# Modulation products in plain float32 on quarters of TensorE's columns, in a two-layer hybrid diffusion block

## The chip, the core and the metric

The kernel runs on one core of a Trainium2 chip. Its five engines are named in the profile's way: PE (TensorE, the matrix engine; PEld its weight loads), DVE (VectorE), ACT (ScalarE), POOL (GpSimd) and SP (SyncE, which only issues transfers here). The metric is the device time of one execution in microseconds, the median of several. A profiled execution also has a span, from its first to its last instruction.

## The reference

Two layers of one trunk work on 256 context tokens and 512 latent tokens of 1024 features, all in float32. Each layer computes a modulation vector of 6 x 1024 values for each of the two token groups from that group's condition (`c` for the latents, `c_ctx` for the context). The six parts are shift, scale and gate of the mixers, and shift, scale and gate of the MLP:

```python
for layer in range(DEPTH):
    ctx_out = layer < DEPTH - 1
    mods = jax.nn.silu(c.astype(f32)) @ mod_w[layer] + mod_b[layer]
    sh1, sc1, gt1, sh2, sc2, gt2 = jnp.split(mods[:, None, :], N_MOD, axis=-1)
    cmods = jnp.split(jax.nn.silu(c_ctx.astype(f32)) @ mod_w[layer] + mod_b[layer], N_MOD)

    p_lat = (rmsnorm(x, norm_mix[layer]) * (1.0 + sc1) + sh1) @ w_in[layer]
    p_ctx = (rmsnorm(ctx, norm_mix[layer]) * (1.0 + cmods[1]) + cmods[0]) @ w_in[layer]
    ...
    x = x + gt1 * (jnp.concatenate([ya_l, yb_l, yc_l], axis=-1) @ w_out[layer])

    h = rmsnorm(x, norm_mlp[layer]) * (1.0 + sc2) + sh2
    x = x + gt2 * sq_relu_mlp(h, mlp_w1[layer], mlp_w2[layer])
    ...
return rmsnorm(x, norm_final)
```

What is left out are the three mixers, S5, gated DeltaNet and RWKV-7, each on its own columns of `p`, and the same steps for the context with `cmods` in layer 0. The products with `mod_w` have only two rows on one side, one for each token group, and 25 MB of weights for each layer on the other.

## The kernel before

Activations are kept with features on the partitions. Dense products (`product`, line 290, whose matmul is line 296) are made exact by splitting both sides into two float32r parts each, high and low: three matmuls in place of one. `weight` (line 265) loads 128 rows by 512 columns of weights into a `wl` tile (line 271), ACT casts the high part into `wh` (line 272), and DVE or POOL subtracts for the low part in `wo` (line 273). Each of the three names has three buffers (`wide`, line 223). Products of plain float32 are two matmul instructions each in the trace.

The order on every engine's queue is made ahead of time: what is emitted has a class of urgency, `CHAIN` (the recurrences) first, then `LEVEL`, `READ`, `PREP`, `S5`, `DENSE`, `FILL`, and a planner places each instruction by modelled times. On an engine the order is then fixed, and an instruction that waits holds all behind it. Tiles of one name are handed out in the order of emission; the banks "d" of PSUM, two of them, serve dense products, modulation and S5 alike.

Modulation is `mods` (line 908). For each group of 512 of the 6144 columns it goes over the eight row tiles of the contraction, sums into one "d" bank, copies the sums to SBUF (line 929), turns them into columns with four transposes (line 932) and adds the bias (line 934). At the start (`eng` None, called at line 1185) four groups of layer 0 are made in plain float32: the weights are loaded to tiles of the arena (line 921), and the stationary side is `sc[:, k]`, two columns (line 922). The projection `front` of layer 0 needs these groups. Everywhere else (`mods` in `run`, line 1195, with 'v') weights are split by `weight` with the low part on DVE, and each row tile takes two float32r matmuls, line 925 with four columns (high and low of both token groups) and line 926 with two; line 936 adds the second pair of rows. There are 20 such groups: six right after the first projection, emitted between pieces of S5 (`next(self.more)`), four ahead of the context's output projection, two inside the context's MLP, and eight in layer 1. All are of class `DENSE`.

The other lines that matter: line 990 loads the tokens, lines 952, 320 and 323 make the norms' reciprocals, 807 to 885 are S5, lines 1708 to 1733 and 1488 to 1511 the recurrences of RWKV-7 and DeltaNet, line 398 and 404 blocks of triangular inverses, line 330 sums over heads, and line 371 and 373 the inverses on DVE.

Of the kernel before, what the change touches and what calls it, by code (L numbers as in the profile page):

```python
# [15 lines left out]
P = 128  # L16
# [8 lines left out]
# tags of small shared tiles: columns, buffers  # L25
# [15 lines left out]
for _n, _w in (("ident", 128), ("lt_f", 128), ("lt_b", 128), ("p_f", 128), ("p_b", 128),  # L41
               ("ones", 128), ("mr", 128), ("rm", 256), ("bo2", 2),
               ("sel2", 128), ("cent", 128), ("bo128", 128), ("scan", 512)):
    CONST[_n] = (_o, _w)
    _o += _w
# [19 lines left out]
class Part:  # L65
    """the context or the latents: first token, tokens, modulation's column."""
# [23 lines left out]
class Kern:  # L90
    def __init__(self, tc, ctx, a, out):
# [13 lines left out]
        self.mr3 = self.mr.rearrange("p (d i) -> p d i", d=2)  # L105
        self.rm3 = self.rm.rearrange("p (d i) -> p d i", d=2)
        self.mhalf = self.cp.tile([P, 12], F32, tag="mhalf", name="mhalf")
# [9 lines left out]
    def prio(self, c):  # L117
        """what is emitted inside is scheduled before the higher classes, in its own order."""
# [33 lines left out]
    def set_rounded(self, count):  # L152
        """makes count of the pages hold float32r."""
# [13 lines left out]
    def own(self, count, late, pieces):  # L167
        """lets what the pieces emit take its tiles from count pages of its own; late: jobs that they outlast."""
# [15 lines left out]
    def s(self, w, p=P, keep=None, kind=None):  # L184
# [12 lines left out]
                # early free, not beside tiles of another life, not across quarters and halves  # L197
# [25 lines left out]
    def wide(self, tag, dt=F32):  # L223
        return self.wp.tile([P, 512], dt, tag=tag, name=self.nm(tag), bufs=3)
# [9 lines left out]
    def load_layer(self, l):  # L234
# [4 lines left out]
        # derived columns  # L239
# [25 lines left out]
    def weight(self, src, eng):  # L265
        """the parts of 128 rows of up to 512 values; eng: the engines that take turns at the low one."""
# [9 lines left out]
    def rows(self, src, eng):  # L276
        """by row tile the parts of 4 x 128 rows of a block of 128 columns."""
# [12 lines left out]
    def product(self, ps, w, acts, first=True, last=True, fresh=False):  # L290
        """ps += sum over k of w[k].T @ act[k]; fresh: the low parts of acts come last."""
# [6 lines left out]
    def dense(self, src, acts, n, eng, fresh=False):  # L298
        """out^T[128 cols, tokens] for one block of 128 columns, in psum."""
# [6 lines left out]
    def rows_rstd(self, ps, n, scale, eps, tag):  # L306
        """(ps * scale + eps) ** -0.5 on a small token-major tile."""
# [7 lines left out]
    def bcast(self, r, w, sel, nt, tag, rt):  # L315
        """r [128 tokens, w per tile] back to feature-major, in psum; rt: scratch."""
# [591 lines left out]
    def mods(self, l, groups, eng):  # L908
# [3 lines left out]
        for g in groups:  # L912
            ps = self.ps("d")
            for k in range(KT):
                if k % 4 == 0:
                    next(self.more, None)
# [1003 lines left out]
```

## Time and profile before

| | |
|---|---|
| time, median of 3 runs | 3077.45 us (3076.12 to 3078.54) |
| span of the profiled execution | 3056.7 us |
| PE busy | 2669.4 us (87%) |
| DVE busy | 1833.7 us (60%) |
| ACT busy | 1186.7 us (39%) |
| POOL busy | 1134.5 us (37%) |
| line 296, all matmuls of dense products | 1424.8 + 915.2 us busy |
| read from and written to memory | 300.76 and 88.90 MB |

The page gives busy time by engine, then the span in 40 slices of 76.4 us with a digit for each (tenths busy; 9 is 90% or more). A matmul's duration holds about 0.17 to 0.2 us in which the next one is already running, so rates are read from one start to the next. Views by line and by stretch, the chain of work that ended last, and the order of time on one engine come from the trace of the same execution.

### The profile page before, as it was taken

How to read it: one execution, taken by the hardware profiler on the slowest of the kernel's cores; microseconds unless marked ns; L12 is line 12 of the kernel's file. 1: busy time of each engine (PE TensorE's matmuls, PEld its weight loads, DVE VectorE, ACT ScalarE, POOL GpSimd, SP SyncE). 2: the span in 40 equal slices, each digit the busy share in tenths (PEclk: the TensorE clock that was granted, in tenths of full speed). 3: DMA queues.
4: the chain of work that ended last, by engine and by line, in shares of the span. 5: the costliest groups of instructions: out<-in, count | busy, mean ns of one | idle time of the engine just before them, and what ended most of it. 6: DMA issues, size and time to landing. Idle time of an engine off the chain costs nothing.

```text
span 3056.7 us, 54445 instructions
## 1 busy us (share of the span) xinstructions
PE 2669.4 (87%) x19956; PEld 2044.2 (67%) x19956; DVE 1833.7 (60%) x4462; ACT 1186.7 (39%) x2411; POOL 1134.5 (37%) x1274
## 2 busy tenths in 40 slices
PE   5789998865898999987899989889887889799998
PEld 1667776543566888876666768667655567477776
DVE  6654878765667756647876562647776753332223
ACT  2344445332534543445423423353334432133332
POOL 2532335424133121123446644344442522244443
PEclk9788999676787999987999999889987859699998
DMA  5345546543653543535233332255555632022222
GB/s 196 96 140 185 151 136 210 154 130 86 200 161 120 166 157 116 167 114 161 85 88 111 125 96 93 102 187 159 148 184 165 211 93 86 28 83 94 93 94 86
DMA packets 324651, 401.73 MB, mean 131 GB/s; under 512 B 142880, under 2 KB 173472, under 8 KB 324256
## 3 DMA queue, kind: packets, MB, share of 16 engines
q1 hardware_dynamic: 324384, 398.24, 41.6%
q8 instruction: 158, 2.59, 0.4%
q14 instruction: 109, 0.89, 0.1%
HBM read 300.76 MB, written 88.90 MB: 127 GB/s over the span
## 4 chain that ended last, share of the span: by engine, by line
PE 53%; DVE 19%; DMA 9%; issue 5%; ACT 4%; SPq 3%; POOL 1%; DVEq 0%; ACTq 0%; POOLq 0%
PE d L296 35%; DMA page<-dr 3%; DVE solve L371 3%; DVE solve L373 3%; PE rc L1733 2%; DVE wo L273 2%; PE rc L1732 2%; PE p L1622 1%; DVE s L472 1%; DMA dr<-page 1%; SPq L352 1%; DMA s<-s 1%; DMA wl<-in_w_dram 1%; ACT wh L272 1%; PE p L481 1%
## 5 line engine op out<-in xcount | busy, mean ns | idle before, releaser
L296 PE MATMUL d<-page,wh 128*128 128x512 f32 (+1 forms) x5024 | 1424.8, 367 | 61.0 <-DVE page L1156 15.5
L296 PEld LDWEIGHTS d<-page,wh 128*128 128x128 f32 x5024 | 919.0, 196 | 234.5 <-DVE page L1156 18.0
L296 PE MATMUL d<-page,wo 128*128 128x512 f32 (+1 forms) x2512 | 915.2, 365 | 5.5 <-DVE wo L273 4.3
L272 ACT CAST wh<-wl 128x512 fp32r<-128x512 f32 (+1 forms) x750 | 457.1, 616 | 710.2 <-PE d L296 421.0
L273 POOL TENSOR_TENSOR wo<-wl,wh 128x512 fp32r<-128x512 f32 (+1 forms) x357 | 471.8, 1325 | 672.0 <-ACT wh L272 635.8
L296 PEld LDWEIGHTS d<-page,wo 128*128 128x128 f32 x2512 | 493.4, 196 | 80.6 <-DVE wo L273 5.8
L273 DVE TENSOR_TENSOR wo<-wl,wh 128x512 fp32r<-128x512 f32 (+1 forms) x393 | 296.1, 758 | 112.6 <-ACT wh L272 104.1
L1156 DVE SCALAR_TENSOR_TENSOR page<-d,mod,page 128x512 f32<-128x512 f32 (+1 forms) x192 | 124.8, 659 | 199.6 <-PE d L296 199.1
L371 DVE TENSOR_TENSOR solve<-solve 128x30 f32<-128x30 f32 (+4 forms) x360 | 151.3, 420 | 21.6 <-issue 12.0
L1147 DVE TENSOR_TENSOR s<-s 128x512 f32<-128x512 f32 (+1 forms) x96 | 60.5, 631 | 172.1 <-ACT s L1146 172.0
L373 DVE TENSOR_TENSOR solve<-solve 128x30 f32<-128x30 f32 (+4 forms) x360 | 142.8, 397 | 7.7
L1499 POOL TENSOR_TENSOR g<-g,gates 64x128 f32<-64x128 f32 x120 | 59.5, 496 | 219.7 <-DVE g L1504 190.4
L285 DVE TENSOR_TENSOR page<-s,page 128x512 fp32r<-128x512 f32 (+1 forms) x118 | 86.6, 738 | 47.5 <-ACT page L284 47.3
L1146 ACT ACTIVATE s<-d 128x512 f32<-128x512 f32 (+1 forms) x96 | 50.6, 527 | 141.5 <-PE d L296 141.4
L472 DVE SCALAR_TENSOR_TENSOR s<-s,ncol,s 128x256 f32<-128x256 f32 (+1 forms) x132 | 96.4, 733 | 3.0
L284 ACT CAST page<-s 128x512 fp32r<-128x512 f32 (+1 forms) x118 | 64.1, 547 | 80.5 <-DVE s L1147 62.9
L926 PE MATMUL d<-wo,scp 128*2 128x512 f32 x160 | 76.3, 477 | 20.6 <-DVE wo L273 19.6
L1622 PE MATMUL p<-page,page 64*128 64x128 f32 (+1 forms) x576 | 84.7, 307 | 10.4 <-DVE page L1625 7.1
L1622 PEld LDWEIGHTS p<-page,page 64*128 64x128 f32 x576 | 73.1, 209 | 27.4 <-issue 12.8
L1733 PE MATMUL rc<-page,page 128*64 128x64 f32 x464 | 86.7, 275 | 2.8 <-DMA page<-dr 2.8
L481 PE MATMUL p<-consts,page 128*128 128x128 f32 x348 | 63.8, 309 | 25.0 <-DMA page<-dr 11.2
L1732 PE MATMUL rc<-page,r 64*64 64x64 f32 x432 | 79.2, 270 | 5.6 <-DVE r L1724 4.0
(464 smaller groups left out, 4057.7 us busy)
## 6 DMA issues: line engine op xcount, KB each, us to landing
wl<-in_w_dram SPq DMA_DIRECT2D x384, 256.0 KB, 2.6
wl<-in_mod_w_dram SPq DMA_DIRECT2D x160, 256.0 KB, 3.0
wl<-in_w_in_dram SPq DMA_DIRECT2D x142, 256.0 KB, 2.9
page<-dr SPq DMA_DIRECT2D x118, 256.0 KB, 3.3
dr<-s SPq DMA_DIRECT2D x72, 256.0 KB, 2.5
dr<-page SPq DMA_DIRECT2D x30, 512.0 KB, 4.1
dr<-page SPq DMA_DIRECT2D x55, 256.0 KB, 2.5
page<-dr SPq DMA_DIRECT2D x16, 834.0 KB, 5.2
```

Of the source, the lines that this page charges most:

```text
L272: nc.scalar.copy(hi, st)
L273: low.tensor_tensor(lo, st, hi.bitcast(F32), OP.subtract)
L285: nc.vector.tensor_tensor(lo, src, hi.bitcast(F32), OP.subtract)
L296: nc.tensor.matmul(ps, x, y, start=(first and i == 0), stop=(last and i == len(order) - 1))
L371: nc.vector.tensor_tensor(tm, y3[:, :j, j:j + 1].to_broadcast([P, j, w]), y3[:, j:j + 1, j + 1:].to_broadcast([P, j, w]), OP.mult)
L373: nc.vector.tensor_tensor(y3[:, :j, j + 1:], y3[:, :j, j + 1:], tm, OP.add)
L472: nc.vector.scalar_tensor_tensor(acc, cp[:, j:j + n], w[:, 5 * i + j:5 * i + j + 1], acc, OP.mult, OP.add)
L481: self.nc.tensor.transpose(p[:, t * 128:(t + 1) * 128], src[:, t * 128:(t + 1) * 128], self.ident)
L1156: nc.vector.scalar_tensor_tensor(x[j], ps, mod[:, 40 + j, g:g + 1], x[j], OP.mult, OP.add)
L1622: nc.tensor.matmul(ps[:, i], flat(bk[d][hs, n0 + i]), kr[d][hs, n0 + i], start=True, stop=True)
L1732: nc.tensor.matmul(o, st[hs, d], kr[d][hs, n, 1], start=True, stop=False)
L1733: nc.tensor.matmul(o, xv[h][:, n, d], self.R[d][:, h, n], start=False, stop=True)
```

## The change

`mods` uses plain float32 everywhere. The stationary side gets 32 columns for each row tile, two with values and 30 of zeros, and four row tiles write to the four quarters of 32 partitions of one bank: the first four row tiles begin the sums there, the other four end them. Each four transfers are issued together, into `wl` tiles (at the start, as before, into tiles of the arena). The copy takes all 128 partitions. In place of transposes come products with a constant `sum4` of 128 by 2, which adds the four quarters as it turns rows to columns. The float32r parts of the conditions go. `wl` has four buffers, `wh` three, `wo` two. The mask `mr` is now read out of `rm`, which holds the same values.

```diff
-               ("ones", 128), ("mr", 128), ("rm", 256), ("bo2", 2),
-               ("sel2", 128), ("cent", 128), ("bo128", 128), ("scan", 512)):
+               ("ones", 128), ("rm", 256), ("bo2", 2),
+               ("sel2", 128), ("cent", 128), ("bo128", 128), ("scan", 512), ("sum4", 2)):
...
+        self.mr3 = self.rm3[:, :, 64:]
...
-        return self.wp.tile([P, 512], dt, tag=tag, name=self.nm(tag), bufs=3)
+        return self.wp.tile([P, 512], dt, tag=tag, name=self.nm(tag), bufs={"wl": 4, "wh": 3, "wo": 2}[tag])
...
-        sg = self.cp.tile([P, KT, 2], F32, tag="sc", name="sc")
+        sg = self.cp.tile([P, KT, 32], F32, tag="sc", name="sc")
+        nc.gpsimd.memset(sg, 0.0)
...
-        parts = self.cp.tile([P, KT, 4], F32R, tag="scp", name="scp")
-        self.split((parts[:, :, 0:2], parts[:, :, 2:4]), sg)
...
-    def mods(self, l, groups, eng):
+    def mods(self, l, groups, arena=False):
...
             ps = self.ps("d")
-            for k in range(KT):
-                if k % 4 == 0:
-                    next(self.more, None)
-                src = self.a["mod_w"][l, g][:, k]
-                if eng is None:
-                    with self.scope():
-                        st = self.s(512)
-                        nc.sync.dma_start(st, src)
-                        nc.tensor.matmul(ps[:2], self.sc[:, k], st, start=(k == 0), stop=(k == KT - 1))
-                    continue
-                hi, lo = self.weight(src, eng)
-                nc.tensor.matmul(ps[:4], self.scp[:, k], hi, start=(k == 0), stop=False)
-                nc.tensor.matmul(ps[:2], self.scp[:, k, 0:2], lo, start=False, stop=(k == KT - 1))
+            for k0 in (0, 4):
+                next(self.more, None)
+                with self.scope():
+                    st = []
+                    for k in range(k0, k0 + 4):
+                        t = self.s(512) if arena else self.wide("wl")
+                        nc.sync.dma_start(t, self.a["mod_w"][l, g][:, k])
+                        st.append(t)
+                    for i, t in enumerate(st):
+                        nc.tensor.matmul(ps[32 * i:32 * i + 32], self.sc[:, k0 + i], t, start=(k0 == 0), stop=(k0 == 4))
             row = self.d(512)
-            r = 2 if eng is None else 4
-            nc.scalar.copy(row[:r], ps[:r])
-            pt = self.ps("d", 4 * r).rearrange("p (j c) -> p j c", j=4)
+            nc.scalar.copy(row, ps)
+            pt = self.ps("d", 8).rearrange("p (j c) -> p j c", j=4)
             for j in range(4):
-                nc.tensor.transpose(pt[:, j], row[:r, j * 128:(j + 1) * 128], self.ident[:r, :r])
+                nc.tensor.matmul(pt[:, j], row[:, j * 128:(j + 1) * 128], self.sum4, start=True, stop=True)
...
-            if eng is not None:
-                nc.vector.tensor_tensor(m, m, pt[:, :, 2:4], OP.add)
...
+    put("sum4", f((i[:, None] % 32) == np.arange(2)[None, :]))
```

## Rows read from the trace of the kernel before

**Rows 1.** The page: busy us of each engine, and PE's slices.

```profile
PE 2669.4 (87%) x19956; PEld 2044.2 (67%) x19956; DVE 1833.7 (60%) x4462; ACT 1186.7 (39%) x2411; POOL 1134.5 (37%) x1274
...
PE   5789998865898999987899989889887889799998
```

**Rows 2.** The table by stretches: us, busy of each engine, granted clock, transfers.

```profile
76.00:452.00 376.00, 344.04 (x2296) 275.24 (x2297) 247.52 (x576) 163.77 (x363) 143.83 (x211) 0.90 0.45 140
452.00:655.00 203.00, 174.08 (x1692) 121.40 (x1692) 161.74 (x454) 94.73 (x209) 94.21 (x111) 0.80 0.56 175
...
750.00:836.00 86.00, 66.92 (x662) 40.55 (x662) 59.21 (x126) 45.10 (x90) 24.63 (x19) 0.70 0.59 190
...
883.00:932.00 49.00, 41.41 (x234) 23.96 (x232) 29.56 (x61) 22.12 (x45) 17.18 (x15) 0.72 0.52 162
...
2230.00:2440.00 210.00, 171.26 (x1671) 111.47 (x1672) 156.81 (x384) 95.33 (x190) 94.91 (x91) 0.82 0.58 182
```

**Rows 3.** PE in order of time, 0 to 80 us: start, length, line, shapes.

```profile
32.95 9.16 PE L922 MATMUL d<-page,sc 128*2 128x512 f32 x16
...
43.11 7.03 PE L922 MATMUL d<-page,sc 128*2 128x512 f32 x16
...
59.28 7.03 PE L922 MATMUL d<-page,sc 128*2 128x512 f32 x16
...
67.03 0.41 PE L932 MATMUL d<-consts,s 2*128 2x2 f32 x4
...
75.59 0.58 PE L296 MATMUL d<-page,wh 128*128 128x256 f32 x1 [0.91 <-ACT page L980]
```

**Rows 4.** Line 921, the loads at the start: issue ns, first and last issue.

```profile
L921 SPq DMA_DIRECT2D page<-in_mod_w_dram x32: 327/328/380, 14.2 to 36.1; - x32
...
DMA to landing us min/median/max: 5.4/5.4/6.1
```

**Rows 5.** PE in order of time, small products and modulation, 440 to 457 us.

```profile
440.07 0.34 PE L1511 MATMUL gc<-page,g 128*64 128x64 f32 x4
...
445.38 0.61 PE L330 MATMUL gc<-consts,page 128*128 128x2 f32 x4
...
449.45 0.33 PE L1733 MATMUL rc<-page,page 128*64 128x64 f32 x2
...
453.35 0.44 PE L404 MATMUL q<-page,page 32*32 32x32 f32 x28
...
454.10 0.25 PE L404 MATMUL q<-page,page 32*32 32x32 f32 x4
...
455.88 0.39 PE L925 MATMUL d<-wh,scp 128*4 128x512 f32 x1
456.11 0.40 PE L926 MATMUL d<-wo,scp 128*2 128x512 f32 x1
```

**Rows 6.** Line 273 alone, sum over the stretches with modulation and 655 to 750.

```profile
sum 643.00, DVE 127.07 POOL 4.39; mean DVE 25.41 POOL 0.88
```

**Rows 7.** The tensor `in_mod_w`: who waited for its loads (us, times), and landing.

```profile
  ACT wh L272: 61.7, 43
...
DMA to landing us min/median/max: 2.5/3.2/7.2
```

**Rows 8.** The chain by line: 452 to 655, 750 to 836, 883 to 932, 2230 to 2440.

```profile
by line: issue 5.7%; DVE solve L371 5.1%; PE p L481 4.5%; DMA page<-dr 4.3%; DVE wo L273 4.3%; DVE solve L373 4.2%; PE rc L1733 3.5%; PE rc L1732 3.4%; PE d L925 3.4%; PE d L926 3.2%; DVE page L1585 2.1%; PE d L841 2.0%; PE q L1439 1.9%; PE
...
by line: PE p L1622 10.7%; issue 8.0%; DVE wo L273 7.8%; DMA solve<-dr 6.9%; PE d L926 6.3%; DMA wl<-in_w_out_dram 5.6%; PE d L925 5.4%; DMA wl<-in_mod_w_dram 4.6%; DMA page<-dr 4.4%; ACT wh L272 3.0%; PE q L1677 2.9%; PE p L1602 2.4%; ACT 
...
by line: PE rc L1733 10.8%; PE rc L1732 10.7%; DMA wl<-in_mod_w_dram 8.4%; DMA wl<-in_w_dram 7.8%; DVE wo L273 7.7%; PE d L926 7.1%; PE d L925 6.6%; DVE s L949 6.5%; PE p L481 4.6%; PE p L1380 4.3%; PE rc L1750 4.2%; issue 3.6%; PE rc L1708
...
by line: DMA page<-dr 8.7%; issue 8.3%; DMA wl<-in_mod_w_dram 8.0%; DMA dr<-page 6.6%; DVE wo L273 6.0%; PE d L885 4.1%; DVE solve L371 3.6%; PE d L926 3.0%; DVE solve L373 2.7%; DMA solve<-dr 2.7%; PE d L925 2.7%; PE rc L1733 2.7%; PE rc L
```

**Rows 9.** The longest waits: engine, line, whom for, us in total, times, longest.

```profile
ACT wh L272 <- PE d L296: 421.0, 225, 5.4
...
PE d L296 <- DVE wo L273: 4.3, 6, 1.1
```

More of the change, by code (lines that the diff above doesn't have):

```diff
@@ L104, in __init__ @@
             setattr(self, n, self.consts[:, o:o + w])
-        self.mr3 = self.mr.rearrange("p (d i) -> p d i", d=2)
         self.rm3 = self.rm.rearrange("p (d i) -> p d i", d=2)
+        self.mr3 = self.rm3[:, :, 64:]
         self.mhalf = self.cp.tile([P, 12], F32, tag="mhalf", name="mhalf")
@@ L897, in silu_c @@
         c = self.d(2 * KT).rearrange("p (k c) -> p k c", k=KT)
-        sg = self.cp.tile([P, KT, 2], F32, tag="sc", name="sc")
+        sg = self.cp.tile([P, KT, 32], F32, tag="sc", name="sc")
+        nc.gpsimd.memset(sg, 0.0)
         nc.sync.dma_start(c, self.a["cT"])
         nc.vector.tensor_scalar(c, c, 0.5, None, OP.mult)
-        nc.scalar.activation(sg, c, AF.Tanh)
-        nc.vector.scalar_tensor_tensor(sg, sg, 1.0, c, OP.add, OP.mult)
-        parts = self.cp.tile([P, KT, 4], F32R, tag="scp", name="scp")
-        self.split((parts[:, :, 0:2], parts[:, :, 2:4]), sg)
-        self.sc, self.scp = sg, parts
-    def mods(self, l, groups, eng):
+        nc.scalar.activation(sg[:, :, 0:2], c, AF.Tanh)
+        nc.vector.scalar_tensor_tensor(sg[:, :, 0:2], sg[:, :, 0:2], 1.0, c, OP.add, OP.mult)
+        self.sc = sg
+    def mods(self, l, groups, arena=False):
         nc = self.nc
@@ L913, in mods @@
             ps = self.ps("d")
-            for k in range(KT):
-                if k % 4 == 0:
-                    next(self.more, None)
-                src = self.a["mod_w"][l, g][:, k]
-                if eng is None:
-                    with self.scope():
-                        st = self.s(512)
-                        nc.sync.dma_start(st, src)
-                        nc.tensor.matmul(ps[:2], self.sc[:, k], st, start=(k == 0), stop=(k == KT - 1))
-                    continue
-                hi, lo = self.weight(src, eng)
-                nc.tensor.matmul(ps[:4], self.scp[:, k], hi, start=(k == 0), stop=False)
-                nc.tensor.matmul(ps[:2], self.scp[:, k, 0:2], lo, start=False, stop=(k == KT - 1))
+            for k0 in (0, 4):
[8 more added lines that the diff above has]
+                        nc.tensor.matmul(ps[32 * i:32 * i + 32], self.sc[:, k0 + i], t, start=(k0 == 0), stop=(k0 == 4))
             row = self.d(512)
-            r = 2 if eng is None else 4
-            nc.scalar.copy(row[:r], ps[:r])
-            pt = self.ps("d", 4 * r).rearrange("p (j c) -> p j c", j=4)
+            nc.scalar.copy(row, ps)
+            pt = self.ps("d", 8).rearrange("p (j c) -> p j c", j=4)
             for j in range(4):
-                nc.tensor.transpose(pt[:, j], row[:r, j * 128:(j + 1) * 128], self.ident[:r, :r])
+                nc.tensor.matmul(pt[:, j], row[:, j * 128:(j + 1) * 128], self.sum4, start=True, stop=True)
             m = mod[:, 4 * g:4 * g + 4]
-            nc.vector.tensor_tensor(m, pt[:, :, 0:2], col["mod_b"][:, 4 * g:4 * g + 4].unsqueeze(2).to_broadcast([P, 4, 2]), OP.add)
-            if eng is not None:
-                nc.vector.tensor_tensor(m, m, pt[:, :, 2:4], OP.add)
+            nc.vector.tensor_tensor(m, pt, col["mod_b"][:, 4 * g:4 * g + 4].unsqueeze(2).to_broadcast([P, 4, 2]), OP.add)
     def rstd(self, x, part):
@@ L1184, in run @@
                 nc.scalar.copy(rs[-1], self.rstd(x, part))
-            self.mods(0, (0, 2, 1, 3), None)
+            self.mods(0, (0, 2, 1, 3), True)
         self.now = 1.5
@@ L1196, in mods @@
             with self.prio(DENSE):
-                self.mods(l, groups, 'v')
+                self.mods(l, groups)
         self.now = 0
@@ L1787, in host_consts @@
     ge = (i[:, None] % 64) >= j[None, :]
-    put("mr", f(np.concatenate([le, ge], 1)))
     lt = (i[:, None] % 64) < j[None, :]
```

## The prediction

> **What bounds the kernel now.** I read the page first: TensorE (PE) is busy 87% of the span, VectorE as the next 60%, and PE's digits fall below 8 in the first two slices, in the 9th and 10th and in a few later ones [rows 1]. The table by stretches then says which stretches the change can reach. Modulation (lines 922, 925 and 926) runs at the start and in four later stretches, 452 to 655, 750 to 836, 883 to 932 and 2230 to 2440 us; there PE is busy 78 to 86% of the time, at a mean granted clock of 0.70 to 0.82 of 2.4 GHz, while from 76 to 452 us it is busy 344 of 376 us [rows 2]. So the projection after the start is held by PE and moves as a whole if it begins earlier, and the other four stretches have idle time that modulation may be the reason for. The chain that ended last, taken for each of these four stretches alone, tells how much of it goes through modulation [rows 8].
>
> **The start.** The program's first projection waits for four groups of modulation. Each group's 16 matmul instructions (8 products of plain float32, two instructions each) take 7.03 us, 0.43 us an instruction; then come a copy and four transposes, and a group starts 8.1 us after the one before (from 43.11 to 59.28 are two) [rows 3]. The 32 transfers are issued between 14.2 and 36.1 us and land 5.4 us after issue, so the last one is there at 41.5 [rows 4], 26 us before the last transposes at 67.03 [rows 3]. The first matmul of the projection starts at 75.59 [rows 3]. The start is thus held by PE's serial products, not by transfers.
>
> **The price of a half group.** The change puts four row tiles on four quarters of the array's columns. No row shows 128x32 float32 products of 512 columns, so I bound them. From above: eight instructions one after another, 8 x 0.43 = 3.44 us. From below: two of 0.43, as if the four were one, 0.87 with a little for the start. Which end is nearer is told by small products: two instructions on 128x64 (one product) take 0.33 us, four of them on the two halves of the columns take 0.34; four instructions on four 32x32 tiles take 0.25 us and 28 take 0.44, 8 ns for each further one [rows 5]. Halves over the full 128 rows run side by side, and four tiles do too, so I take 0.87. Today the same four row tiles cost eight float32r products of 0.23 us from start to start, 1.84 us [rows 5].
>
> A rule of the Trainium skill speaks for a little more: TensorE: Matmul & The Clock Gate, Part 3, gives four packed row tiles a measured 3.07 times, not 4. By that a half group would be an estimated 3.44 / 3.07 = 1.12 us, and the sum below would be 6 us later. The rows with 64 columns show no such loss, so the sum keeps 0.87.
>
> **Other parts of the edit.** Four transposes of 4 rows (0.41 us together [rows 3]) become four products of 128 rows by 2 columns, eight instructions. The nearest row is four instructions 128x128 on 2 columns in 0.61 us [rows 5]; eight take at least 0.61 and at most twice that, 1.22. I take 1.22, as nothing shares the array with them: +0.81 a group. The copy of the sums to SBUF keeps its width of 512 columns and only has more partitions: nothing. In 20 groups 160 casts on ScalarE (ACT) and 160 low parts on VectorE (DVE) go; the low parts are nearly all of the 127 us that line 273 spends on DVE in the stretches of modulation [rows 6]. The second addition to `mod`, the zeroing of 256 columns of `sc` while GpSimd is idle, 126 columns less of constants and the mask read out of `rm` are small or hidden behind the first transfers: nothing.
>
> **Buffers.** `wl` gets four buffers, `wo` two. For the dense products a low part may now start only when the last but one block of weights is used up. PE now waits for low parts in line 296 for 4.3 us in all, while ACT waits 421 us for `wh` to come free from those products [rows 9]. So casts are already held by PE three blocks back, and the low part, 0.7 us later, will be held two blocks back: a block of 512 tokens is 12 products, 12 x 0.23 = 2.8 us, in which a low part fits, 0.69 us on DVE or 1.3 on GpSimd. From -5 us (the fourth `wl` lets transfers go out earlier) to +10 (twice PE's present waits, and some DVE work queued behind a waiting low part); I take 0.
>
> **The waits that are added.** PE itself now waits for each transfer of modulation; behind that wait in its queue stand the products of the two recurrences and their preparation. SyncE (SP) cannot issue the next four until four products have freed their `wl`, and behind it stand the recurrences' own loads. Landing takes 2.5 to 7.2 us, 3.2 in the median [rows 7]. The price for 40 half groups is between 0 (the planner has placed them after the landing) and 40 x 3.2 = 128 us. The nearest row is today's chain, where these transfers hold 4.6% of 86, 8.4% of 49 and 8.0% of 210 us, 25 us [rows 8]. I take 25.
>
> **The sum.** On today's chain in the four stretches [rows 8]: products of lines 925 and 926, 6.6% of 203, 11.7% of 86, 13.7% of 49, 5.7% of 210, 42 us; low parts and casts 4.3%, 10.8%, 7.7% and 6.0%, 34 us; transfers 25 us; 101 us together. All 320 products take 320 x 0.23 = 74 us, so 57% of them is on the chain. With the change: 40 x 0.87 = 35 us of products, 57% is 20; transposes 20 x 0.81 = 16, 57% is 9; transfers 25. That is 54 in place of 101, 47 less. What is late next is the recurrences and S5, which hold the other 70 to 90% of these chains, so not all of it arrives; I take three quarters, 35 us (from a quarter, 12, to all of it). At the start the four groups go at 2 x 0.87 + 1.22 + 0.7 (from a group's last product, 59.28 + 7.03 = 66.3, to its transposes at 67.03 [rows 3]) = 3.7 us each: 32.95 + 14.6 = 47.6, and the last landing at 41.5 allows 45. That is 20 us before 67.03, from 16, if the norm is then held up by the S5 tables on DVE, to 24, if transposes and products of different groups overlap. Together 55 us. The profiled span was 3056.7 us, the median 3077.45, 21 more; the span after should be 3002 and the time **3022**.
>
> **Rivals.** (a) More comes through: all 47, 24 at the start, and in 452 to 655, where DVE is busy 162 of 203 us [rows 2], half of the 48 low parts x 0.79 = 38 us shortens S5: 47 + 24 + 19 = 90, 2987. Against it: the other work of that stretch is mostly latency. (b) Only the start counts, since recurrences and S5 set the other stretches: 3077 - 20 = 3057. (c) Slower: PE stands for transfers. The half group can't be issued while the one before it holds `wl`, so each may cost the landing. The gain is gone when a half group holds the chain for (25 + 55) / 40 = 2.0 us; halfway from there to the median landing, at 2.6 us, it is 40 x 2.6 - 25 = 79 us more than I took, 3101. For it: casts wait for exactly these transfers 61.7 us in 43 waits [rows 7]. Against it: those waits are 0.4 us per tile. (d) The quarters don't run side by side: products on the chain 40 x 3.44 x 0.57 = 78 in place of 20, nothing at the start, 47 - 58 = -11: 3088.
>
> For (d) a sentence of the Trainium skill can be read: in TensorE: Matmul & The Clock Gate, Part 3, weight loads pass running products only where the rows' group differs, and the four quarters share all rows. By that rule (d) would hold; the rows on 128x64 [rows 5] disagree, as two halves with the same rows take the time of one.
>
> **How the numbers follow.** Forecast 0.56, (a) 0.13, (b) 0.12, (c) 0.10, (d) 0.05, and 0.04 that gains and waits cancel. About 0.2%, 6 us, is what a measurement can tell from no change. Faster 0.56 + 0.13 + 0.12 = 0.81, same 0.04, slower 0.15. The order on each queue is planned anew, which no row prices. The forecast's own range is 2990 to 3050; to leave out no more than 2 in 10 it has to reach (a), (b) and (d): 2975 to 3090.
>
> **What would show it.** Right: line 922 in four blocks of about 1.8 us, and the first matmul of line 296 near 55 us; pairs of modulation's instructions starting within some 10 ns; no cast or low part for modulation; the four stretches shorter, above all 750 to 836; no new waits of DVE or GpSimd for PE at line 273. Wrong: half groups of 2 us or more; PE waiting for `in_mod_w` for over 80 us in all; the projection still starting near 75; or stretches as long as now with DVE idler.

## The result, and the profile after

The changed kernel takes 3022.74 us (median, 3012.89 to 3029.64) against 3076.78 us before: a ratio of 0.984, 95% interval 0.980 to 0.987 (40 to 61 us), or 54 us less by the medians where 55 were predicted. The profiled execution took 3012.89 us, its span is 3011.1; so it is the fastest of the four, 10 us below their median. Line 296 of the dense products is unchanged in it; modulation is now lines 920 (transfers), 923 (products), 925 (copy), 928 (products with `sum4`) and 930 (bias).

The page of the changed kernel, busy times and PE's slices, belongs beside [rows 1]:

```profile
PE 2663.1 (88%) x20052; PEld 2044.2 (68%) x20052; DVE 1725.7 (57%) x4281; ACT 1096.4 (36%) x2250; POOL 1122.3 (37%) x1275
...
PE   5889998876899999987889999888888889799998
```

DVE lost 108 us and ACT 90, as the change says; PE lost only 6. The table by stretches of the changed kernel belongs beside [rows 2] (us; busy time of PE, PEld, DVE, ACT and POOL with instructions; granted clock, share of the DMA engines, GB/s):

```profile
448.00:639.00 191.00, 162.29 (x1504) 108.52 (x1502) 122.91 (x364) 62.90 (x147) 81.39 (x101) 0.78 0.58 178
...
730.00:807.00 77.00, 64.23 (x630) 38.27 (x630) 43.79 (x106) 29.42 (x61) 25.05 (x20) 0.84 0.66 216
844.00:875.00 31.00, 30.39 (x240) 16.21 (x238) 11.75 (x38) 8.52 (x19) 12.53 (x13) 1.00 0.56 174
2190.00:2410.00 220.00, 187.42 (x1807) 118.56 (x1805) 119.08 (x323) 63.74 (x133) 90.53 (x97) 0.86 0.61 188
```

The four stretches that hold later modulation groups lasted 203, 86, 49 and 210 us before and last 191, 77, 31 and 220 now: the gain is in the first three, and the last one is longer.

PE in order of time from 32 to 64 us in the changed kernel belongs beside [rows 3] (start, length, then what; x is the number of instructions; in brackets the idle time before and what ended it):

```profile
32.19 3.64 PE L923 MATMUL d<-page,sc 128*32 128x512 f32 x16
36.61 1.05 PE L928 MATMUL d<-consts,s 128*128 128x2 f32 x8 [0.78 <-ACT s L925]
37.59 1.92 PE L923 MATMUL d<-page,sc 128*32 128x512 f32 x16
40.30 1.05 PE L928 MATMUL d<-consts,s 128*128 128x2 f32 x8 [0.78 <-ACT s L925]
41.28 1.92 PE L923 MATMUL d<-page,sc 128*32 128x512 f32 x16
46.39 1.59 PE L928 MATMUL d<-consts,s 128*128 128x2 f32 x8 [3.18 <-ACT s L925]
47.91 3.64 PE L923 MATMUL d<-page,sc 128*32 128x512 f32 x16
52.55 1.84 PE L928 MATMUL d<-consts,s 128*128 128x2 f32 x8 [1.00 <-DVE mod L930]
...
63.22 0.58 PE L296 MATMUL d<-page,wh 128*128 128x256 f32 x1 [2.00 <-ACT page L974]
```

Two of the four groups take 1.92 us for 16 instructions where 7.03 stood: side by side works, 0.87 us for a half group once the tail of about 0.17 is taken off. The fourth takes 3.64, at a granted clock of 0.50 (47.9 to 51.6 us). The first takes 3.64 too; the view gives 1.00 there, but the trace's record of the clock begins only at 36.5 us, so the clock of the first group isn't shown. The projection starts 12.4 us earlier, not 20. And it ends when it ended before, as its matmuls of line 296 on the high parts show (the kernel before, the changed one, and the run with the new start alone that follows below; count, lengths in ns, first and last start):

```profile
L296 PE MATMUL d<-page,wh x864: 276/388/793, 75.6 to 448.7; 128*128 128x256 f32 x89, 128*128 128x512 f32 x84
```

```profile
L296 PE MATMUL d<-page,wh x864: 276/388/795, 63.2 to 448.1; 128*128 128x256 f32 x87, 128*128 128x512 f32 x86
```

```profile
L296 PE MATMUL d<-page,wh x864: 276/388/795, 64.4 to 436.7; 128*128 128x512 f32 x87, 128*128 128x256 f32 x86
```

From first to last start that is 373 us before, 385 in the changed kernel and 372 with the start alone. The number of buffers goes with it: in the profiled executions of all fourteen kernels of this text the projection takes 372 to 375 us in the five that have three buffers of each name, and 375 to 385 in the nine that have four, three and two.

In the later stretches it looks different. PE from 730 to 745 us, changed kernel:

```profile
730.83 1.06 PE L923 MATMUL d<-wl,sc 128*32 128x512 f32 x8
734.66 1.04 PE L923 MATMUL d<-wl,sc 128*32 128x512 f32 x2 [2.77 <-DMA wl<-in_mod_w_dram]
736.36 3.27 PE L923 MATMUL d<-wl,sc 128*32 128x512 f32 x6 [0.65 <-DMA wl<-in_mod_w_dram]
740.31 1.05 PE L928 MATMUL d<-consts,s 128*128 128x2 f32 x8 [0.68 <-ACT s L925]
741.29 1.05 PE L923 MATMUL d<-wl,sc 128*32 128x512 f32 x4
743.10 2.58 PE L923 MATMUL d<-wl,sc 128*32 128x512 f32 x4 [0.76 <-DMA wl<-in_mod_w_dram]
```

The first half group finds its four tiles landed: eight instructions in 1.06 us. The second doesn't: one product starts when its tile lands and takes the time of four (x2, 1.04), and the other three follow one by one as theirs land (x6, 3.27). The third is split in two. The loads of that second half group were asked for when the first had freed the four `wl` tiles, at the end of its products (730.83 + 1.06; SyncE's queue):

```profile
731.90 1.06 SPq L920 DMA_DIRECT2D wl<-in_mod_w_dram  x2
```

A half group that follows another at once thus has a landing of its own to wait for, here 2.77 us of idle PE. More than four `wl` buffers weren't tried. Over all 40 half groups there are 87 such pieces. What that makes, in the table by stretches from 300 us to the end for modulation's matmuls alone (PE's busy time is the fourth number; the first row is the kernel before, the second the changed one):

```profile
300.00:3000.00 2700.00, 120.05 (x320) 24.06 (x320) 0.00 (x0) 0.00 (x0) 0.88 0.42 130
```

```profile
300.00:3000.00 2700.00, 109.47 (x320) 14.30 (x320) 0.00 (x0) 0.00 (x0) 0.00 (x0) 0.89 0.43 130
```

So a half group holds PE for 3.0 us before and 2.7 after, where the prediction had 1.84 and 0.87. The waits of PE for those transfers, and of others for PE, in the changed kernel (engine and line, releaser: us in total, times, longest; the first line is of line 923 alone, with PE's weight loads):

```profile
  DMA wl<-in_mod_w_dram: 32.4, 21
```

```profile
POOL wo L273 <- PE d L296: 520.9, 239, 48.5
ACT wh L272 <- PE d L296: 391.1, 212, 8.5
...
SPq L920 <- PE d L923: 129.9, 56, 12.7
```

GpSimd's low parts, which before waited for their cast, now wait for PE to free `wo` (see [rows 9]). SyncE stands 130 us for `wl` tiles that PE hasn't read yet, as foreseen.

### The profile page after: what moved, and what is told of

It is laid out like the page before. It is cut to its first block, busy times and chain, and to the rows that moved or that the text cites. A ratio compares the mean times of both kernels' runs of the same rounds, so it can differ in the third digit from the quotient of the medians.

```text
span 3011.1 us, 54432 instructions
## 1 busy us (share of the span) xinstructions
PE 2663.1 (88%) x20052; PEld 2044.2 (68%) x20052; DVE 1725.7 (57%) x4281; ACT 1096.4 (36%) x2250; POOL 1122.3 (37%) x1275
## 5 line engine op out<-in xcount | busy, mean ns | idle before, releaser
L273 POOL TENSOR_TENSOR wo<-wl,wh 128x512 fp32r<-128x512 f32 (+1 forms) x357 | 481.0, 1348 | 670.0 <-PE d L296 520.9
L272 ACT CAST wh<-wl 128x512 fp32r<-128x512 f32 (+1 forms) x590 | 360.2, 616 | 553.9 <-PE d L296 391.1
L273 DVE TENSOR_TENSOR wo<-wl,wh 128x512 fp32r<-128x512 f32 (+1 forms) x233 | 167.4, 720 | 105.1 <-PE d L296 41.5
L1141 DVE TENSOR_TENSOR s<-s 128x512 f32<-128x512 f32 (+1 forms) x96 | 82.3, 858 | 158.8 <-ACT s L1140 155.8
L923 PE MATMUL d<-wl,sc 128*32 128x512 f32 x320 | 109.5, 717 | 14.3 <-DMA wl<-in_mod_w_dram 12.8
L472 DVE SCALAR_TENSOR_TENSOR s<-s,ncol,s 128x512 f32<-128x512 f32 (+1 forms) x132 | 93.8, 713 | 2.8
L1704 DVE TENSOR_TENSOR page<-page,rc 64x128 f32<-64x128 f32 x144 | 40.9, 284 | 78.8 <-PE rc L1702 73.5
L481 PE MATMUL p<-consts,page 128*128 128x128 f32 x348 | 63.7, 306 | 24.6 <-ACT page L1642 9.6
```

What stands on the lines that cost most here:

```text
L272: nc.scalar.copy(hi, st)
L273: low.tensor_tensor(lo, st, hi.bitcast(F32), OP.subtract)
L472: nc.vector.scalar_tensor_tensor(acc, cp[:, j:j + n], w[:, 5 * i + j:5 * i + j + 1], acc, OP.mult, OP.add)
L923: nc.tensor.matmul(ps[32 * i:32 * i + 32], self.sc[:, k0 + i], t, start=(k0 == 0), stop=(k0 == 4))
L1141: nc.vector.tensor_tensor(r, r, r, OP.mult)
```

## The experiments

Each is given with its median, that of the kernel before on the same chip, and the ratio with its interval. "First products" are those at the start, "later groups" the 20 others.

**The new modulation at the start alone** (later groups split as before, three buffers of each name):

```diff
-        return self.wp.tile([P, 512], dt, tag=tag, name=self.nm(tag), bufs={"wl": 4, "wh": 3, "wo": 2}[tag])
+        return self.wp.tile([P, 512], dt, tag=tag, name=self.nm(tag), bufs=3)
...
-                self.mods(l, groups)
+                self.mods_old(l, groups, 'v')
...
```

> The new modulation at the start alone; the 20 later groups as before, all three weight tiles with three buffers. Theory A (from comparing the two traces: the first projection begins 12 us earlier but ends at the same time, the first recurrence is 8 us earlier): 8 us faster than before, 3069. Theory B (the forecast's own accounting, the projection moves as a whole): 20 us faster, 3057.

Measured: 3017.51 us against 3069.03, ratio 0.985 [0.982, 0.989]. The start alone gains as much as the whole change, more than either theory gave it. Its projection starts at 64.4 us, 11 earlier than before, and ends 12 earlier.

**The later groups alone**, with the four buffers of `wl`:

```diff
-            self.mods(0, (0, 2, 1, 3), True)
+            self.mods_first(0, (0, 2, 1, 3))
...
```

(`mods_first` is the start as it was before.)

> The new modulation in the 20 later groups alone; the four at the start serial, with two columns, as before; buffers as after. Theory A: nearly all of the gain is here, 46 us faster than before, 3031. Theory B: 35 us faster, 3042.

Measured: 3043.36 against 3069.03, 0.992 [0.990, 0.995], 26 us less. The two halves together would make 77, and the change makes 54: they don't add. Seen from this run, the new start brings the remaining 21 us by the medians, 26 by the ratios.

**The kernel before with the buffers of the change:**

```diff
-        return self.wp.tile([P, 512], dt, tag=tag, name=self.nm(tag), bufs=3)
+        return self.wp.tile([P, 512], dt, tag=tag, name=self.nm(tag), bufs={"wl": 4, "wh": 3, "wo": 2}[tag])
```

> The kernel before with four wl, three wh and two wo, nothing else. Forecast: 0, between 5 us faster and 10 slower, 3072 to 3087. Rival: the new waits of GpSimd for PE at the low part (521 us in 239 in the kernel after, none to speak of before) hold something up, 15 us or more slower, over 3092.

Measured: 3047.84 against 3069.03, 0.994 [0.991, 0.996], 21 us less, though its trace shows the wait that was feared (waits of line 273, first in the kernel before, then with these buffers):

```profile
POOL wo L273 <- ACT wh L272: 635.8, 276, 48.8
```

```profile
POOL wo L273 <- PE d L296: 548.6, 243, 50.4
DVE wo L273 <- PE d L296: 51.4, 44, 7.0
```

So the wait costs little, and something gains 21 us: a forecast of nothing, and a rival on the other side, both missed. The later groups alone had these buffers too, so most of their 26 us can't be put down to the new products.

**All products of a half group on the first quarter**, one after another, 32 rows copied and summed:

```diff
-                        nc.tensor.matmul(ps[32 * i:32 * i + 32], self.sc[:, k0 + i], t, start=(k0 == 0), stop=(k0 == 4))
+                        nc.tensor.matmul(ps[:32], self.sc[:, k0 + i], t, start=(k0 + i == 0), stop=(k0 + i == 7))
...
```

> The kernel after with all eight row tiles of a group summed on the first quarter, so that no two products run side by side: 3.44 us for a half group. Theory A (in the later stretches products went in 87 pieces of 0.87 us, 1.9 us a half group, hardly cheaper than before, and PE is not what holds those stretches): the start's 8 us and little more is lost, 3030 to 3045. Theory B (57% of the products' time is on the path): 40 x (3.44 - 1.9) x 0.57 = 35 and the start's 20, 3077.

Measured: 3054.86 against 3069.03, 0.996 [0.994, 0.999]; 14 us less than before, so side by side, at the start and later, is worth 32 us of the 54 by the medians and 38 by the ratios (0.996 less 0.984). Its second group at the start, and modulation's matmuls after 300 us (PE in order of time; the table by stretches):

```profile
42.64 7.05 PE L923 MATMUL d<-page,sc 128*32 128x512 f32 x16
```

```profile
300.00:3000.00 2700.00, 170.13 (x320) 30.09 (x320) 0.00 (x0) 0.00 (x0) 0.00 (x0) 0.89 0.43 130
```

7.05 us against 1.92 for the same 16 instructions on four quarters; with the tail taken off, four times. PE has 61 us more to do in the later groups than in the changed kernel, and the first projection starts at 78.8, 15.6 later: 76 us together, of which about half arrives at the end.

**Three orders that change nothing else.** The kernel before with its first four groups in another order, the kernel before with the six groups after the projection in another order, and the changed kernel with its first four in another order:

```diff
-            self.mods(0, (0, 2, 1, 3), None)
+            self.mods(0, (2, 0, 3, 1), None)
```

```diff
-            mods(0, *range(4, 4 + 6))
+            mods(0, 9, 8, 7, 6, 5, 4)
```

```diff
-            self.mods(0, (0, 2, 1, 3), True)
+            self.mods(0, (2, 0, 3, 1), True)
```

> The kernel before with the four groups at the start in the order 2, 0, 3, 1 in place of 0, 2, 1, 3: the same instructions, transfers and sizes, and the projection still needs all four. The three runs so far don't add up (start alone -51 us, the other groups with their buffers -26, the buffers alone -21, all together -52). Theory N (the plan made anew moves the time by itself): this edit, which takes nothing away and adds nothing, moves the median by 10 to 25 us to either side, and milestones of the middle stretches move by as much, though the first projection starts at 75 us as before. Theory C (each of the gains has a cause in its edit): within 6 us of the kernel before.

> The kernel before with the six groups after the first projection in the order 9 to 4 in place of 4 to 9; the first use of any of them comes long after all six are done. Again nothing is taken away or added. Theory N: 10 to 25 us to either side. Theory C: within 6 us.

> The changed kernel with the four groups at the start in the order 2, 0, 3, 1. Theory N: 10 to 25 us to either side of the changed kernel, so its 54 us is one draw of several. Theory C: within 6 us of it, 0.984 of the kernel before.

Measured: 3050.21, 3069.95 and 3017.16 against 3066.43; 0.994 [0.991, 0.997], 1.001 [0.9995, 1.003] and 0.983 [0.977, 0.988]. One neutral edit of two moved the kernel before by 16 us, though its projection starts at 75.1 as before; the changed kernel can't be told from what it was, its four runs lying between 2998 and 3037. A difference of 15 to 20 us between two plans of this kernel thus needs no cause in the edit beyond the new order, and the buffers' 21 are hardly more than that. The change's 54 is well above. But with both kernels in the order 2, 0, 3, 1 the change is worth 33 us by the medians (3050.21 to 3017.16), 35 by the ratios, with the wide interval of the last run. How much it gains seems to depend on the order that it is measured in.

**The casts and low parts put back**, their results unused:

```diff
                         nc.sync.dma_start(t, self.a["mod_w"][l, g][:, k])
+                        if not arena:
+                            hi, lo = self.wide("wh", F32R), self.wide("wo", F32R)
+                            nc.scalar.copy(hi, t)
+                            nc.vector.tensor_tensor(lo, t, hi.bitcast(F32), OP.subtract)
```

> The changed kernel, with a cast to high parts on ScalarE and a subtraction for low parts on VectorE for each of the 160 weight tiles of the later groups, whose results nothing uses (so it does work that is left over, and the products are those of the change). It gives back what the change took from these two engines and nothing else. Theory A (what the later stretches gained is the casts and low parts that left the chain, 34 us of it in the sum): 20 to 35 us slower than the changed kernel, about 0.992. Theory T (the later stretches gained from the transfers issued four at a time into four buffers, as the run with the buffers alone suggests): within 8 us of the changed kernel, 0.984 to 0.987.

Measured: 3060.52 against 3066.43, 0.997 [0.995, 0.999], 1.3% above the changed kernel, some 40 us. What was put back (groups of instructions, busy us and mean ns of one, then the idle time before them):

```profile
L925 DVE TENSOR_TENSOR wo<-wl,wh 128x512 fp32r<-128x512 f32 x160 | 121.9, 773 | 56.4 <-ACT wh L924 49.5 <-PE d L296 5.1 <-POOL page L149 0.6
...
L924 ACT CAST wh<-wl 128x512 fp32r<-128x512 f32 x160 | 97.9, 619 | 136.7 <-DMA wl<-in_mod_w_dram 108.3 <-DVE page L836 12.6 <-DVE wo L925 7.3
```

122 us on DVE and 98 on ACT, and the queue of ACT stands 108 us for transfers besides. By amount, a third of the DVE time arrives at the end. PE's own time in modulation is 117.35 us, 8 more than without, so it isn't the products that make this loss. But most of it doesn't arise beside the casts. In the two profiled executions this run is 9 us ahead of the changed kernel at the first sum of the context's output projection (798.0 and 807.3), when ten of the 20 groups are done; 13 behind at the end of layer 0 (1904.2 and 1890.8), with only two groups in between; 23 behind after S5 of layer 1 (2326.6 and 2303.5), and 41 at layer 1's output projection (2531.1 and 2490.5), though its last group is done at 2411.7. And the run with the start alone keeps all 160 casts and low parts, for products that need them, and is as fast as the changed kernel. So it isn't shown that the casts as such cost the 40 us; the plan made anew around them is a rival that no run takes away.

**The last landed tile first.** The four products issued in the order 3, 2, 1, 0:

```diff
-                    for i, t in enumerate(st):
+                    for i, t in reversed(list(enumerate(st))):
```

> The changed kernel, with the four products of a half group issued in the order of the row tiles 3, 2, 1, 0 in place of 0, 1, 2, 3. The transfers are issued in the order 0 to 3, so the first product waits for the last one and the other three find theirs landed: the wait is the same, but the four start together. In the changed kernel the 160 later products run in 87 pieces of 0.87 to 1.06 us, 1.9 us for a half group. Theory P (the price of the pieces is on the chain): pieces fall to about 40, PE has 40 x 1.0 = 40 us less to do, and half of that arrives, 20 us less than the changed kernel, 0.977 of the kernel before. Theory N (transfers and the new plan decide, the pieces lie in time that PE has idle): pieces fall as well, and the time is within 10 us of the changed kernel.

Measured: 3032.1 against 3068.38, 0.988 [0.985, 0.990]; no gain on the changed kernel's 0.984, rather 10 us lost. PE's order of time from 731 to 741 us with it, its modulation after 300 us, and the stretch 730 to 850 us, in that order:

```profile
731.28 1.06 PE L923 MATMUL d<-wl,sc 128*32 128x512 f32 x8 [0.21 <-ACT page L886]
739.05 1.93 PE L923 MATMUL d<-wl,sc 128*32 128x512 f32 x8 [6.71 <-DMA wl<-in_mod_w_dram]
```

```profile
300.00:3000.00 2700.00, 70.95 (x320) 8.18 (x320) 0.00 (x0) 0.00 (x0) 0.00 (x0) 0.85 0.42 130
```

```profile
730.00:850.00 120.00, 95.05 (x981) 70.00 (x980) 59.73 (x152) 38.05 (x77) 28.23 (x28) 0.70 0.57 175
```

The same stretch in the changed kernel:

```profile
730.00:850.00 120.00, 106.43 (x1156) 72.67 (x1154) 69.60 (x177) 41.25 (x82) 36.18 (x37) 0.90 0.62 193
```

Most half groups do go four wide, 45 pieces in place of 87, and PE spends 38 us less on them. But PE idles until the last transfer (6.71 us at 739.05), the granted clock of the stretch is 0.70 in place of 0.90, and at the lower level (1.2 GHz, granted 0.50 from 739 to 741 us) eight instructions take 1.93 and not 1.06. (The two stretches are the same in time, not in work; from 730 us to the first sum of the context's output projection the clock is 0.62 here, to 825 us, and 0.84 in the changed kernel, to 807.) Over all executions its mean granted clock is 0.863, the changed kernel's 0.883. The page of the profiled execution, the slowest of its four, gives PE 2682.8 us busy in all, 20 more than the changed kernel, with 38 less of modulation: 58 us more went to other work. The gain that the theory of the pieces' price forecast didn't come. As the turned order also made waits longer and the clock lower, it doesn't show what the pieces cost by themselves.

**The same, with four groups moved forward**, from the context's output projection to the six groups after the first projection:

```diff
             mods(0, *range(4, 4 + 6))
+            mods(1, 0, 2, 1, 3)
...
-            mods(1, 0, 2, 1, 3)
```

> The run before, and the four groups 0, 2, 1, 3 of layer 1, which are now emitted right before the context's output projection, are emitted before it with the six groups 4 to 9 of layer 0, in the stretch 640 to 730 us in which PE of the changed kernel is busy 62 of 91 us. Of the 77 us between the end of S5 and the context's output projection (730 to 807) these four groups fill a part. Theory A (these groups, not the recurrences, hold the context's output projection): it starts 20 us or more before 807 and the time falls by 15 to 30 us against the run with the turned order alone. Theory B (S5 and the recurrences of that stretch are held by PE just as much): S5 ends as much later, and the time is within 10 us of that run.

Measured: 3100.94 against 3068.38, 1.010 [1.008, 1.013], 69 us slower than the run it was compared with. Neither theory holds. The four groups are done at 690 us in place of 807, S5 ends at 722 in place of 730, and the first product of the context's output projection starts at 752 in place of 810, but its first sum is at 825 in both: that sum wasn't held by these groups. The loss is in the recurrence. One of its matmul lines from 545 to 1000 us in the two kernels, the last-first kernel ahead (first and last start stand at the end):

```profile
L1702 PE MATMUL rc<-r,page x88: 218/218/366, 623.4 to 901.5; 64*64 64x64 f32 x88
```

```profile
L1702 PE MATMUL rc<-r,page x88: 218/218/366, 738.0 to 985.1; 64*64 64x64 f32 x88
```

The third step starts 115 us later, and the steps that follow end 84 later. Each half group also asks for the next piece of S5 where it is emitted, so pieces of S5 moved forward with the groups; which of the two pushed the recurrence back isn't told apart.

**No transfers for the later groups:**

```diff
-                        t = self.s(512) if arena else self.wide("wl")
-                        nc.sync.dma_start(t, self.a["mod_w"][l, g][:, k])
+                        if arena:
+                            t = self.s(512)
+                            nc.sync.dma_start(t, self.a["mod_w"][l, g][:, k])
+                        else:
+                            t = self.consts[:, 0:512]
```

> The changed kernel, leaving out the transfers of modulation's weights in the 20 later groups: their products read constants that are in SBUF from the start (so those modulation values are other ones). Products, copies, sums and additions stay. Theory A (the waits for transfers cost what PE shows, 32 us in 21 waits, and the pieces 40 us more of PE): 25 to 45 us less than the changed kernel. Theory T (PE and SP stand for these transfers with all that is queued behind them, as in rival (c)): 60 us less or more. Theory 0 (the transfers lie beside other work): within 12 us of the changed kernel.

Measured: 2970.95 against 3068.38, 0.968 [0.966, 0.971]: 97 us below before, about 50 below the changed kernel. That lies between the two theories, just above the first. Modulation's matmuls in it:

```profile
300.00:3000.00 2700.00, 56.68 (x320) 10.25 (x320) 0.00 (x0) 0.00 (x0) 0.00 (x0) 0.88 0.38 115
```

With nothing to wait for, a half group takes 1.4 us of PE. The products fall by 53 us and the waits by 32, 85 in all, and 50 arrive. As the run with the last tile first took 38 us off the products and gained nothing, though with longer waits, the waits, and what stands behind them in PE's and SyncE's queues, may be the larger part of these 50; the two weren't taken away one by one.

**The start alone, in another order** (the edit beside that of the start alone):

```diff
-            self.mods(0, (0, 2, 1, 3), True)
+            self.mods(0, (2, 0, 3, 1), True)
```

> The run with the new modulation at the start alone (three buffers of each name, later groups as before), with its four groups in the order 2, 0, 3, 1. That edit alone moved the kernel before by -16 us and the changed one by about -4. The first such run was 51 us faster than before, though its projection starts 11 us and ends 12 us earlier only. Theory N (the rest of the 51 is the plan made anew): this run is 12 to 35 us faster than before, 0.989 to 0.996. Theory C (an earlier start sets free more than its 12 us later on): 45 to 55 us faster again, 0.982 to 0.9855.

Measured: 3021.71 against 3068.38, 0.983 [0.982, 0.985]. The start's gain came back with another order: 45 to 52 us against the kernel before, where its projection starts 11 to 13 us earlier. Against the kernel before in the same order 2, 0, 3, 1 (3050.21) it is 28 us by the medians and 33 by the ratios. In both orders the start alone has nearly all that the change has: 51 of 54, and 28 of 33.

**Where the time goes along the run.** Starts of a few instructions, us, one profiled execution each. The executions of the kernel before and of the changed one are fast ones, some 18 and 10 us below their medians; those of the neutral order and of the two starts lie within 1 us of theirs, that of the run without transfers 4 below. Differences of under 10 us against the changed kernel's column thus say little.

| | before | before, other order | start alone | start alone, other order | changed | no transfers |
|---|---|---|---|---|---|---|
| first projection, line 296 | 75.6 | 75.1 | 64.4 | 62.6 | 63.2 | 63.7 |
| first step of RWKV-7's recurrence | 413.6 | 413.7 | 402.4 | 400.5 | 405.7 | 400.9 |
| context's output projection, first sum | 844.9 | 840.3 | 839.3 | 829.5 | 807.3 | 735.4 |
| latents' MLP of layer 0, last sum | 1930.0 | 1917.7 | 1903.9 | 1907.3 | 1890.8 | 1839.7 |
| S5 of layer 1, last product | 2359.9 | 2343.0 | 2315.2 | 2317.0 | 2303.5 | 2246.1 |
| layer 1's output projection, first sum | 2532.2 | 2522.0 | 2493.4 | 2494.5 | 2490.5 | 2442.0 |
| last sum of the last MLP | 3038.6 | 3030.3 | 2998.7 | 3002.1 | 2994.1 | 2947.4 |

Two readings. The start's 11 to 13 us arrive at the recurrence and stay; against the neutral order, which is the fairer one, the two kernels with the new start alone are 10 to 14 us ahead at the end of layer 0 and 26 to 28 ahead after S5 of layer 1, where nothing was changed. And the later groups gain at first: the changed kernel is 22 to 32 us ahead of the start alone at the context's output projection. It is 13 to 17 ahead at the end of layer 0, 12 to 14 after S5 of layer 1, 3 to 4 at layer 1's output projection and 5 to 8 at the end. What the later groups gain is given back step by step. The 9 us or so that are lost between S5 of layer 1 and its output projection go in a stretch that holds the last four of the eight groups of layer 1 and what comes after them.

## Why the prediction came out right

The number and the sign were right, and so were the bounds; the split was not. One step of the sum was no step: the 21 us between the profiled span and the median. In every later run span and time of one execution differ by 2 us; the profiled execution before was, by that, only a fast one of some 3058 us. The span after was 3011.1 and not 3002.

**The start, 20 of the 55.** The serial products were what held it, and the price of a half group, 0.87 us, is confirmed. But the projection came 12.4 us earlier. The step that failed is 3.7 us a group, taken as if nothing but PE, at the higher clock, stood in it: from one group's start to the next, and to the end of the last one's `sum4` products, they took 5.4, 3.7, 6.6 and 6.5 us. The first group's products take 3.64 us; that it was slower than the others stood in [rows 3], with 9.16 us against 7.03. The third group's copy waits 3.18 us behind S5's copies on ACT, the fourth group's products then run at half the clock (3.64 us), its `sum4` products wait a microsecond for DVE, and its bias is added at 59.8, 5.4 us after them, behind S5's tables on DVE. The lower end of the term, 16, named those tables and was still too high. The other premise, that the projection moves as a whole, holds for the start alone (12 us earlier at its end), but not in the changed kernel: 12.4 us at its beginning are 0.6 at its end and 8 at the recurrence. In the median, though, the start alone is worth 45 to 52 us, 28 to 33 in the other order, and 21 to 26 beside the new later groups. Of that 12 are seen at the recurrence; a neutral order of the same groups is worth 16 by itself; the rest appears in layer 1, and what sets it free isn't settled.

**The products, 42 to 20 on the chain.** This is the term that was mis-sized. PE was busy with them for 120 us before and 109 after, the tail of each piece counted; the sum had 74 and 35. Two things were left out: that a quarter can't start before its own tile lands, so that one early product costs what four do (x2 in 1.04 us), and that PE had been running these stretches at mean clocks of 0.70 to 0.82 [rows 2]. Of the order in which they may start the Trainium skill says, in TensorE: Matmul & The Clock Gate, Part 3, that matmuls start and end strictly in the order of the queue. The trace of the run with the last tile first agrees: three of the four tiles had landed at 735.2, 735.9 and 738.3 us, and all four products start at 739.05, behind the one whose tile came last.

**Casts and low parts, 34 to 0.** They are gone, as forecast; what that was worth isn't shown. The run that puts them back is some 40 us slower, which fits in size, but loses most of it where few casts or none are, and the start alone keeps them all and loses nothing.

**Transfers, 25 to 25.** PE waits 32.4 us for them, below the 80 that would have told against the forecast. Taken away with the pieces they cause, they are worth 50, so the term was probably too small; waits and pieces weren't told apart. Rival (c) was at work in part, without reaching its deciding point: a half group does hold PE for 2.7 us, more than the 2.0 named there, but it held it for 3.0 before, which the rival's price had at 1.84.

**Transposes**, taken at 1.22 us for eight instructions: 1.05, and 1.59 to 1.84 in the two groups at the start that meet the lower clock.

**Buffers, taken at nothing.** "No new waits at line 273" was wrong: GpSimd's wait moved from the cast to PE (520.9 us). PE in turn waits for low parts 13.3 us, in the changed kernel's group of line 296:

```profile
L296 PE MATMUL d<-page,wo 128*128 128x512 f32 (+1 forms) x2512 | 917.7, 366 | 13.7 <-POOL wo L273 7.4 <-DVE wo L273 5.9
```

Before it was 5.4: the 4.3 of the working were VectorE's alone, and GpSimd's were 1.1. That is 8 us, within the upper end of +10. The longer first projection, 375 to 385 us with the new buffers and 372 to 375 without, is a price that the working didn't have either; so is, the other way, the 21 us gained by the buffers alone, hardly more than a neutral order moves.

**Three quarters arrive.** Of the later groups' 47, 35 were to arrive at the end. By themselves they bring 26, of which their buffers alone bring 21, and beside the new start about nothing. The assumption that failed is that the start and the later stretches add up: the start brought more than its 20, the later groups less than their 35, and the two misses cancelled. That the total fits was in part luck, and so was the order that was measured: the other one gives 33 to 35 us.

**The rivals.** (b), the start alone: right about what counts, wrong about the price, 3017 to 3022 and not 3057. (d), no side by side: the run with the products one after another gives 3055, not 3088, and the products at the start show that the quarters do run together, with 1.92 us for 16 instructions against 7.05. The sentence of the Trainium skill that was read for (d), in TensorE: Matmul & The Clock Gate, Part 3, has weight loads pass running products only where the rows' group differs. The trace disagrees for quarters of the columns: all eight weight loads of a half group that share all rows lie within 0.16 us from 730.83, while its first products run for 0.62 us. (a) needed more to come through than did.

## What to carry to other kernels

Products packed side by side save PE's time only if all their operands are there when the first one is issued (1.4 us a half group without transfers, 2.7 with them): count pieces between landings, not instructions, and look at the clock that a longer wait leaves behind before turning the order round. In a kernel whose order is planned as a whole, measure an edit that changes nothing but the order before giving a cause to 20 us, and try parts both alone and together, since gains of separate stretches need not add. Put the control of an edit in the same order as the edit: here that took the change from 54 us to about 35. And look where along the run a difference arises before giving it to the work that was put in or taken out.

## What the runs showed of the hardware that was not expected

Four plain float32 products with 32 stationary columns each, on four quarters of the columns and over the same 128 rows, take the time of one: 1.92 us for 16 instructions against 7.05 one after another, nearly four times with the tail of 0.17 us taken off both. A single one that starts alone takes as long as the four (x2 in 1.04 us, x8 in 1.06). The same eight take 1.93 us behind a wait of 6.71 us, at the lower of the two clocks (granted 0.50). The first of these was forecast from smaller products; the others weren't.
